# Moving a query projection of a hybrid attention layer from the solve into the attention slots

## The chip, the cores and the metric

The kernel runs on one core of one Trainium2 chip. The metric is device time in microseconds (us) of one execution. The core has a matmul engine (TensorE, in the rows PE, with its weight loads as PEld), VectorE (DVE), ScalarE (ACT) and GpSimd (POOL), and SyncE (SP), whose work here is to issue DMA transfers. Each engine takes its instructions from a queue of its own; semaphores make an instruction wait for one on another engine.

## The reference

The reference runs two layers over 256 latent tokens and 256 context tokens of width 1024. Each layer is half a SwiGLU step, a token mixer, and half a SwiGLU step, each followed by a layer norm. The change touches the mixer of layer 0 alone. That mixer has two groups of heads side by side:

```
h = modulated tokens (512 x 1024)
A (8 heads of 64):  q, k, v = h @ w; rotary on the latent rows of q and k
    latent rows:  softmax over a window of 128 on either side, all context keys, and a sink logit
    context rows: softmax over the context keys and the sink
B (4 heads of 128, forward and backward): q, k, v, z, gates = h @ w
    q, k, v = silu(short_conv(.)) of five taps along the tokens; q and k normalised
    gated delta rule: a state S per head, S <- decay * (S - beta k (k.S)) + beta k v, read out by q
    out = norm(read-out) * silu(z)
x = layernorm(alpha * x + gate * (concat(A, B) @ w_out))
```

All of it is float32 arithmetic.

## The kernel before

**Products.** A float32 matrix is split into a high part (`wh`, `ht_hi`, cast on ACT, or on DVE and POOL) and the remainder (`wl`, `ht_lo`, a subtraction on DVE or POOL). A product is three matmuls: high by high (L391), low by high (L393) and high by low (L394). A projection of 128 columns over 512 tokens is 24 matmuls that fill one PSUM bank.

**Order.** The program is written in Python as a list of operations. A scheduling pass then fixes, before anything runs, the order of the instructions on every engine. So an edit in the source moves instructions on all engines, and within an engine the order stands: what waits holds up all that is behind it. Buffers come from small pools with tags: a projection asks for "a bank with tag pm", gets the oldest, and waits until the last reader of what was in it is done.

**First part of the mixer, `ab_proj`.** PSUM is divided into banks pm (two), x (two), g, q, and r (two). PE computes the k projections of the four B heads (`pproj`, the latent half first, the context half when its transposes are ready), the gate projection (`pg`, 16 rows, in bank g), the four q projections (the first in bank q, the others in pm), and then four z projections. Each k and q projection goes through `ab_conv`: the middle tap on ACT (L901), four taps on DVE (L912), silu on ACT (L916). The bank is free when the last tap is done. The results are transposed on PE (`pkt`, `pqt`), their squares are summed on ACT, and POOL raises the sums to a power (`rk`, `rki`, `rq`, L938). `pgt` is the transpose of the gates. `pG` and `pQ` are the Gram matrices of head 0 (keys by keys, and queries by keys). Between them DVE applies the last layer norm's weight and bias to the rows of the residual (L330, eight operations of 128x1024, tiles r0 and r1), and POOL sends the rows to a store (`xs`), because the space of r0 and r1 is used for the A queries (`qTa`) and keys (`kk`) later.

**Second part, `ab_late`.** The Gram matrices of all heads are weighted and transposed, and go through a store (`scr_out`) into the tile W of DVE, which solves a triangular system in 31 steps of two operations (`ab_solve`, L1177 and L1181, result X). While DVE solves, PE makes the A queries of heads 0 to 3 (`ab_attn_proj(0)`: four steps `pat`, each a product of 128 tokens by 256 columns, a rotary product on DVE and POOL for the latent tokens, a transpose `pqT`), the four v projections (banks g and q in turn) and the A queries of heads 4 to 7 (`ab_attn_proj(1)`). DVE puts the taps of the v convolutions between the solve's steps. Two of the v's have one tap on ACT and POOL (L909, L910). X then goes through a store (`scr_in`) into the tile `xv`.

**Third part.** PSUM is divided anew into banks O (two), sc (two) and dn (four). The A attention runs in 35 pipelined slots (`attn_a`): the query is split on ACT and POOL (`qs`, L1294 and L1295), PE makes scores (`pS`), DVE takes the maximum (L1313), ACT the exponential (L1318), DVE divides (L1322), PE transposes (`pP`, "turn") and multiplies by the values (`pOa`). These slots lie between the steps that turn X into the inverses of the blocks (`delta_inverse`: `pN`, `pZ`, with DVE's transposes `z` of `xv`) and then between the steps of the scan over the tokens (`delta_scan`).

The functions that the change touches:

## Time and profile before

| | us |
|---|---|
| median of three runs | 1801.73 (1801.4 to 1803.04) |
| the profiled execution | 1802.69 |
| its span | 1800.3 |
| PE busy in the span | 1757.1 (98%) |
| DVE busy in the span | 1239.4 (69%) |

Times in the rows count from the start of the span. The span is the part of the execution between the first and the last recorded instruction; 2.4 us lie around it. "PEclk" is the share of PE's full clock that was granted in a stretch: 1.00 is 2.4 GHz, and 0.50 is 1.2 GHz. A number in square brackets behind a row is the time that the engine stood idle before it, and behind the arrow what ended that. A name in the rows is the tile in the program, with the number of the buffer left out.

### The profile page before, as it was taken

The page shows a single profiled execution, that of the slowest core. Times are in us where ns is not written, and L with a number is a line of the kernel's source. Part 1 is how long each engine was busy: PE and PEld are TensorE (multiplying, and loading weights), DVE is VectorE, ACT ScalarE, POOL GpSimd, SP SyncE. Part 2 cuts the span into 40 slices and gives each one's busy share as a digit, 9 for nine tenths or more (in the row PEclk, how much of TensorE's full clock was granted, in tenths as well). Part 3 has the DMA queues.
Part 4 walks back from the last instruction along what each step waited for, and adds up shares of the span by engine and source line. Part 5 has one row for each costly group of instructions (what it writes and reads, how often), then busy time and mean ns, then how long its engine had stood idle before and what let it go on. Part 6 is the DMA issues. An engine that isn't in the chain of part 4 may idle for free. (4 is left out here: it accounts for less than half of the span.)

```text
span 1800.3 us, 24410 instructions
## 1 busy us (share of the span) xinstructions
PE 1757.1 (98%) x9571; PEld 1481.2 (82%) x9571; DVE 1239.4 (69%) x1956; ACT 670.4 (37%) x1176; POOL 180.5 (10%) x296
## 2 busy tenths in 40 slices
PE   6999999999998999999999999999999999999997
PEld 2978878878797988987887888878878889889997
DVE  2784864867778785897674436885756769777556
ACT  2432232224654663342331222522332225655442
POOL 1000000002242310200000002000000023010000
PEclk9999999999999999999999999999999999999999
DMA  9564543623241123375452223662653524146652
GB/s 350 190 211 139 187 164 119 222 60 119 89 125 63 56 77 110 131 244 187 160 169 94 94 96 139 197 223 95 206 192 105 199 81 161 36 162 224 196 177 96
DMA packets 178173, 267.56 MB, mean 149 GB/s; under 512 B 14639, under 2 KB 126683, under 8 KB 177547
## 3 DMA queue, kind: packets, MB, share of 16 engines
q1 hardware_dynamic: 172944, 250.58, 41.9%
q0 software_dynamic: 4624, 14.29, 2.4%
q8 instruction: 75, 1.23, 0.3%
q10 hardware_dynamic: 491, 1.15, 0.2%
q14 instruction: 39, 0.32, 0.1%
HBM read 259.64 MB, written 6.34 MB: 148 GB/s over the span
## 5 line engine op out<-in xcount | busy, mean ns | idle before, releaser
L374 ACT ACTIVATE wh<-wr 128x1024 fp32r<-128x1024 f32 (+1 forms) x311 | 325.4, 1057 | 790.8 <-PE pgu L393 307.0
L376 DVE TENSOR_TENSOR wl<-wr,wh 128x1024 fp32r<-128x1024 f32 (+1 forms) x311 | 375.5, 1219 | 220.8 <-ACT wh L374 217.3
L391 PE MATMUL pgu<-ht_hi,wh 128*128 128x512 f32 (+1 forms) x1472 | 516.1, 353 | 3.5 <-ACT h L266 3.5
L393 PE MATMUL pgu<-ht_lo,wh 128*128 128x512 f32 (+1 forms) x1472 | 518.1, 353 | 0.5 <-POOL ht_lo L269 0.5
L394 PE MATMUL pgu<-ht_hi,wl 128*128 128x512 f32 (+1 forms) x1472 | 517.9, 353 | 0.1
L391 PEld LDWEIGHTS pgu<-ht_hi,wh 128*128 128x128 f32 x1472 | 277.6, 190 | 43.5 <-ACT h L266 3.8
L393 PEld LDWEIGHTS pgu<-ht_lo,wh 128*128 128x128 f32 x1472 | 278.9, 190 | 38.5 <-POOL ht_lo L269 0.9
L394 PEld LDWEIGHTS pgu<-ht_hi,wl 128*128 128x128 f32 x1472 | 278.9, 190 | 37.9 <-DVE wl L376 0.3
L170 DVE SCALAR_TENSOR_TENSOR acc<-wa,cv,acc 128x1024 f32<-128x1024 f32 x224 | 272.8, 1279 | 0.0
L393 PE MATMUL pdn<-wl,hhi 128*128 128x512 f32 (+1 forms) x622 | 240.9, 388 | 0.0
L391 PE MATMUL pdn<-wh,hhi 128*128 128x512 f32 (+1 forms) x622 | 239.9, 390 | 0.0
L394 PE MATMUL pdn<-wh,hlo 128*128 128x512 f32 (+1 forms) x622 | 239.2, 388 | 0.0
L391 PEld LDWEIGHTS pdn<-wh,hhi 128*128 128x128 f32 x622 | 116.6, 188 | 32.4 <-issue 7.5
L394 PEld LDWEIGHTS pdn<-wh,hlo 128*128 128x128 f32 x622 | 116.8, 188 | 23.8
L393 PEld LDWEIGHTS pdn<-wl,hhi 128*128 128x128 f32 x622 | 116.8, 188 | 23.5
L440 DVE TENSOR_TENSOR sg<-sg,pgu 128x512 f32<-128x512 f32 (+1 forms) x86 | 53.6, 623 | 109.0 <-PE pgu L394 105.0
L625 DVE SCALAR_TENSOR_TENSOR tm<-pdn,gate 128x512 f32<-128x512 f32 (+1 forms) x98 | 64.3, 675 | 61.2 <-PE pdn L394 61.1
L439 ACT ACTIVATE sg<-pgu 128x512 f32<-128x512 f32 (+1 forms) x86 | 46.0, 535 | 66.2 <-PE pgu L394 66.2
L198 POOL DMA_DIRECT2D gsc<-rows x12 | 6.2, 524 | 628.0 <-DVE rows L181 628.0
L441 ACT ACTIVATE hhi<-sg 128x512 fp32r<-128x512 f32 (+1 forms) x86 | 49.5, 576 | 35.2 <-DVE sg L440 35.2
L442 DVE TENSOR_TENSOR hlo<-sg,hhi 128x512 fp32r<-128x512 f32 (+1 forms) x86 | 53.6, 624 | 12.2 <-ACT hhi L441 12.2
L394 PE MATMUL pproj<-ht_hi,wl 128*128 128x512 f32 (+1 forms) x160 | 56.1, 355 | 0.0
(383 smaller groups left out, 2203.9 us busy)
## 6 DMA issues: line engine op xcount, KB each, us to landing
wr<-in_ffn_w_gu_dram SPq DMA_DIRECT2D x84, 1024.0 KB
wa<-in_ada_w_dram SPq DMA_DIRECT2D x144, 512.0 KB
wr<-in_ffn_w_down_dram SPq DMA_DIRECT2D x40, 1024.0 KB
wr<-in_ab_w_in_dram SPq DMA_DIRECT2D x11, 1024.0 KB
wr<-in_c_w_in_dram SPq DMA_DIRECT2D x6, 1024.0 KB
gate<-gsc POOLq DMA_DIRECT2D x10, 512.0 KB, 4.9
wr<-in_ffn_w_gu_dram SPq DMA_DIRECT2D x8, 512.0 KB
wr<-in_ffn_w_down_dram SPq DMA_DIRECT2D x8, 512.0 KB
```

Source lines behind the costliest of these rows:

```text
L170: i = nc.vector.scalar_tensor_tensor(out=acc[:, sl], in0=wa[:, sl], scalar=cv, in1=acc[:, sl], op0=ALU.mult, op1=ALU.add)
L198: nc.gpsimd.dma_start(out=self.gsc[m // 3, :, h * 512:(h + 1) * 512], in_=rows[32 * g:32 * g + 2, :])
L374: self.last_high = nc.scalar.activation(out=hv, in_=raw, func=AF.Copy)
L376: self.last_split = (eng or nc.vector).tensor_tensor(out=lv, in0=raw, in1=hv.bitcast(F32), op=ALU.subtract)
L391: self.first_mm = nc.tensor.matmul(out=out, lhsT=lhs[0], rhs=rhs[0], start=start, stop=False)
L393: self.link(nc.tensor.matmul(out=out, lhsT=lhs[0], rhs=rhs[1], start=False, stop=False))
L394: self.last_mm = nc.tensor.matmul(out=out, lhsT=lhs[1], rhs=rhs[0], start=False, stop=stop)
L439: nc.scalar.activation(out=sg, in_=pts[0][:, :NT], func=AF.Silu)
L440: nc.vector.tensor_tensor(out=sg, in0=sg, in1=pts[1][:, :NT], op=ALU.mult)
L441: nc.scalar.activation(out=h_hi[:, c, :], in_=sg, func=AF.Copy)
L442: self.evacuated = nc.vector.tensor_tensor(out=h_lo[:, c, :], in0=sg, in1=h_hi[:, c, :].bitcast(F32), op=ALU.subtract)
L625: i = nc.vector.scalar_tensor_tensor(out=tm, in0=pt[:, cs], scalar=mul, in1=self.gate[:, t // 2, ds], op0=ALU.mult, op1=ALU.mult)
```

## The change

The banks of the four k projections, the places of the eight row operations and of the two transfers to the store, and the last query projection with what hangs on it are moved. No arithmetic is added or taken out. The projection `ab_attn_proj(1)` runs its steps in the order of tokens 2, 3, 0, 1 in banks dn, one behind each of the first four attention slots; its temporaries lie in the tiles of the inverse (`va`, `z`). v3 is written into a part of `qTa`, transposed in a bank dn, and its exponentials' order is set by `last_silu`. The solve's product tile is `sT` instead of one of its own. The attention slots take heads 0 to 3 of two blocks of tokens first, so that the first eight need no query of heads 4 to 7.

```diff
--- before.py
+++ after.py
@@ -913,10 +913,11 @@
                 out=av[:, :, t0:t1], in0=pv[:, :, t0 + o:t1 + o], scalar=w(j), in1=av[:, :, t0:t1],
                 op0=ALU.mult, op1=ALU.add,
             )
-        self.after(nc.scalar.activation(out=dst, in_=a, func=AF.Silu), hold)
-
-    def ab_tok(self, src, name):
-        pt = self.bank("x", name)
+        self.last_silu = nc.scalar.activation(out=dst, in_=a, func=AF.Silu)
+        self.after(self.last_silu, hold)
+
+    def ab_tok(self, src, name, tag="x"):
+        pt = self.bank(tag, name)
         for tb in range(4):
             self.nc.tensor.transpose(
                 out=pt[:, tb * 128:(tb + 1) * 128], in_=src[:, tb * 128:(tb + 1) * 128], identity=self.ident
@@ -993,7 +994,7 @@
         need(3)
         pts = []
         for n in range(4):
-            pts.append(self.bank("r" if n > 1 else "pm", "pproj"))
+            pts.append(self.bank("rrgq"[n], "pproj"))
             self.proj(pts[n], *ws[n], (0, LAT))
         self.start_context()
         for n in range(4):
@@ -1024,9 +1025,10 @@
                 )
             if h == 1:
                 rows()
-            self.next_affine(2, self.convolved)
-            if h % 2:
-                nc.gpsimd.dma_start(out=self.xs[:, h - 1:h + 1], in_=self.rows[h // 2])
+            if h:
+                self.next_affine(2, self.convolved)
+            if h == 2:
+                nc.gpsimd.dma_start(out=self.xs[:, 0:2], in_=self.rows[0])
 
         for h in range(4):
             pt = chunk(9 + h)
@@ -1041,6 +1043,8 @@
                 exps()
             self.ab_gram(h)
             if h == 0:
+                self.next_affine(2, self.weighed)
+                nc.gpsimd.dma_start(out=self.xs[:, 2:4], in_=self.rows[1])
                 self.vt = L.tile([P, 4, 4, P], F32, tag="gate", name="vt", bufs=1)
         self.ab_pow(self.rq, ssq, -0.5)
         V.tensor_scalar(out=self.rq, in0=self.rq, scalar1=float(P) ** -0.5, scalar2=None, op0=ALU.mult)
@@ -1063,8 +1067,8 @@
             for x in range(2):
                 wv.append(self.split_w(raw[:, :, P * x:P * x + P], aw if p else False))
 
-        def v_tok(h):
-            pv = self.ab_tok(vTs[h], "pvt")
+        def v_tok(h, tag="x"):
+            pv = self.ab_tok(vTs[h], "pvt", tag)
             V.tensor_tensor(
                 out=vt[:, :, h, :], in0=pv.rearrange("p (t x) -> p t x", t=4),
                 in1=rki[:, :, h].unsqueeze(2).to_broadcast([P, 4, P]), op=ALU.mult,
@@ -1073,7 +1077,8 @@
         def value(h):
             pt = self.bank("q" if h % 2 else "g", "pproj")
             self.proj(pt, *wv[h], (0, TOK))
-            vTs.append(self.tmp("sq"))
+
+            vTs.append(self.qT[:, 3, :] if h == 3 else self.tmp("sq"))
             self.ab_conv(pt, 8 + h, vTs[h], [self.last_exp], (0,) if h > 1 else ())
             zt = self.tmp("m")
             nc.sync.dma_start(out=zt, in_=self.zscr[h])
@@ -1096,11 +1101,8 @@
                 self.after(self.last_load, [self.W_load])
             value(h)
             self.ab_solve(3)
-        for i, f in enumerate(self.ab_attn_proj(1, weights[1])):
-            f()
-            if i == 0:
-                v_tok(3)
-                self.ab_solve(3)
+        self.ab_solve(3)
+        return weights[1], lambda: v_tok(3, "dn")
 
     def ab_gram(self, h):
 
@@ -1144,7 +1146,7 @@
                     out=self.AT[u][:, tb, :], in0=pG[:, tb * P:(tb + 1) * P], scalar=self.a2[:, tb, u:u + 1],
                     in1=E3[:, tb, :], op0=ALU.mult, op1=ALU.mult,
                 )
-            V.tensor_tensor(out=self.PT[u].rearrange("p t x -> p (t x)"), in0=pQ, in1=E, op=ALU.mult)
+            self.weighed = V.tensor_tensor(out=self.PT[u].rearrange("p t x -> p (t x)"), in0=pQ, in1=E, op=ALU.mult)
             src = self.AT[u]
             if d == 1:
                 sT = self.tmp("sT")
@@ -1173,7 +1175,7 @@
         V, W, X = nc.vector, self.W, self.X
         for j in range(self.solved, min(self.solved + n, 31)):
             m, k = j + 1, 31 - j
-            pv = self.aw.tile([P, 256], F32, tag="prd", name="prd", bufs=1)[:, 0:m * k].rearrange("p (a b) -> p a b", a=m)
+            pv = self.tmp("sT")[:, 0:m * k].rearrange("p (a b) -> p a b", a=m)
             V.tensor_tensor(
                 out=pv, in0=X[:, 0:m, j:j + 1].to_broadcast([P, m, k]),
                 in1=W[:, j:j + 1, j + 1:32].to_broadcast([P, m, k]), op=ALU.mult,
@@ -1197,12 +1199,12 @@
         raw = self.load_w(w[:, :, 256 * p:256 * p + 256])
         return [self.split_w(raw[:, 4 * x:4 * x + 4, :], pool, eng) for x in range(2)]
 
-    def ab_attn_proj(self, p, ws):
+    def ab_attn_proj(self, p, ws, banks=("pm", "x"), tags=("m", "m"), order=range(4)):
 
         nc, io, P = self.nc, self.io, 128
         V = nc.vector
         rope = self.rope
-        tmp = lambda: self.tmp("m")
+        tmp = lambda: self.tmp(tags[0])
 
         def rot(dst, src, tb, n):
 
@@ -1210,7 +1212,7 @@
                 nc.scalar.activation(out=dst, in_=src, func=AF.Copy)
                 return
             co, si = (rope[:, tb, i, :].unsqueeze(1).to_broadcast([P, n, 32]) for i in range(2))
-            t = tmp()
+            t = self.tmp(tags[1])
             t1 = t[:, 0:32 * n].rearrange("p (h x) -> p h x", h=n)
             t2 = t[:, 256:256 + 32 * n].rearrange("p (h x) -> p h x", h=n)
             x1, x2 = src[:, :, 0:32], src[:, :, 32:64]
@@ -1227,7 +1229,7 @@
 
         def step(tb):
             sl = slice(tb * P, (tb + 1) * P)
-            pt = self.bank("pm", "pat")
+            pt = self.bank(banks[0], "pat")
             for k in range(KD):
                 hv, lv = ws[k // 4]
                 self.mm3(
@@ -1239,7 +1241,7 @@
                 rot(q.rearrange("p (h x) -> p h x", h=4), pt[:, 0:256].rearrange("p (h x) -> p h x", h=4), tb, 4)
 
                 def finish(sl=sl, q=q):
-                    pq = self.bank("x", "pqT")
+                    pq = self.bank(banks[1], "pqT")
                     for c in range(2):
                         nc.tensor.transpose(
                             out=pq[:, c * P:(c + 1) * P], in_=q[:, c * P:(c + 1) * P], identity=self.ident
@@ -1269,7 +1271,7 @@
                 done.pop()()
             done.append(finish)
 
-        return [lambda tb=tb: step(tb) for tb in range(4)] + [lambda: done.pop()()]
+        return [lambda tb=tb: step(tb) for tb in order] + [lambda: done.pop()()]
 
     def split_o(self, c, sl, src):
 
@@ -1283,7 +1285,7 @@
 
         nc, P = self.nc, 128
         V = nc.vector
-        items = [(tb, h) for tb in (2, 3, 0, 1) for h in range(8)]
+        items = [(tb, h) for g in ((2, 3), (0, 1)) for h4 in (0, 4) for tb in g for h in range(h4, h4 + 4)]
         state = {}
 
         def query(tb, h):
@@ -1315,7 +1317,8 @@
                 out=st[:, 2:3], in0=st[:, 0:1], scalar=-0.125, in1=self.nsink[:, h:h + 1], op0=ALU.mult, op1=ALU.min
             )
             pe = self.tmp("pexp")[:, 0:nk]
-            nc.scalar.activation(out=pe, in_=s, func=AF.Exp, scale=0.125, bias=st[:, 2:3], accum_out=st[:, 3:4])
+            i = nc.scalar.activation(out=pe, in_=s, func=AF.Exp, scale=0.125, bias=st[:, 2:3], accum_out=st[:, 3:4])
+            self.after(i, [self.last_silu])
             nc.scalar.activation(out=st[:, 4:5], in_=self.sink[:, h:h + 1], func=AF.Exp, bias=st[:, 2:3])
             V.tensor_tensor(out=st[:, 5:6], in0=st[:, 3:4], in1=st[:, 4:5], op=ALU.add)
             V.reciprocal(out=st[:, 6:7], in_=st[:, 5:6])
@@ -1601,12 +1604,19 @@
                     self.ctx_tag, self.lnpool = "x", self.long
                     with self.phase_pool("aw") as self.aw, self.temps(cacc=2, sq=2, sT=1, m=3):
                         self.ab_proj()
-                        self.ab_late(self.aw)
+                        aw, last_values = self.ab_late(self.aw)
                     self.ctx_tag, self.lnpool = "dn", None
-                self.new_ht()
                 st.enter_context(self.psum(O=2, sc=2, dn=4))
                 with self.temps(z=2, va=2, o=3, pexp=3, pT=3):
+
                     att = self.attn_a()
+                    for f in self.ab_attn_proj(1, aw, ("dn", "dn"), ("va", "z"), (2, 3, 0, 1)):
+                        if len(att) > 31:
+                            att.pop(0)()
+                        f()
+                        if last_values:
+                            last_values = last_values()
+                    self.new_ht()
                     inv = self.delta_inverse()
                     for i, f in enumerate(inv):
                         f()
```

On PE, between the k projections' last matmuls and the gate projection. Before (`pproj` first k, then `pg`):

```order
L394 MATMUL pproj<-ht_hi,wl 128x256
L391 MATMUL pproj<-ht_hi,wh 128x256
L393 MATMUL pproj<-ht_lo,wh 128x256
L394 MATMUL pproj<-ht_hi,wl 128x256
L393 MATMUL pg<-ht_lo,wh 16x512
L394 MATMUL pg<-ht_hi,wl 16x512
```

After, on PE at the beginning of the gate projection (the `pproj` rows are the end of q2):

```order
L393 MATMUL pproj<-ht_lo,wh 128x512
L394 MATMUL pproj<-ht_hi,wl 128x512
L922 MATMUL pkt<-ident,skT 128x128 x8
L391 MATMUL pg<-ht_hi,wh 16x512
L393 MATMUL pg<-ht_lo,wh 16x512
L394 MATMUL pg<-ht_hi,wl 16x512
```

The gate projection moved from directly behind the k projections to behind q1, q2 and two key transposes.

On DVE, around the copy of the gates (`gt`) and the taps of q0 and q1 (`cacc`). Before:

```order
L830 COPY gt<-pgt 128x64
L833 TENSOR_TENSOR gy<-gt,hd 128x32
L912 SCALAR_TENSOR_TENSOR cacc<-pproj,cwc,cacc 128x2x254
L834 SCALAR_TENSOR_TENSOR gu<-gy 128x32
L912 SCALAR_TENSOR_TENSOR cacc<-pproj,cwc,cacc 128x2x255
L849 TENSOR_SCALAR gy<-gy 128x32
L376 TENSOR_TENSOR wl<-wr,wh 128x1024
```

After, on DVE at the same copy:

```order
L830 COPY gt<-pgt 128x64
L833 TENSOR_TENSOR gy<-gt,hd 128x32
L1020 TENSOR_TENSOR rk<-rk 128x16
L834 SCALAR_TENSOR_TENSOR gu<-gy 128x32
L838 TENSOR_SCALAR beta<-beta 128x32
L849 TENSOR_SCALAR gy<-gy 128x32
L839 RECIPROCAL beta<-beta 128x32
L1021 TENSOR_TENSOR a_2964<-beta,rk 128x32
L912 SCALAR_TENSOR_TENSOR cacc<-pproj,cwc,cacc 128x2x254 x2
L841 TENSOR_SCALAR gs<-gu 128x32
L912 SCALAR_TENSOR_TENSOR cacc<-pproj,cwc,cacc 128x2x255 x2
```

The square of `rk` moved ahead of the taps of q0 and q1, which now come two and two.

On PE, from the last v projection to the inverse. Before (`pat` and `pqT` are the query projection, `pvt` the transpose of v3):

```order
L394 MATMUL pat<-wh,ht_lo 128x256
L921 MATMUL pvt<-ident,sq 128x128 x4
L1244 MATMUL pqT<-ident,m 128x128 x8
L1511 MATMUL pO_5494<-identR,zeroR 128x512
L1511 MATMUL pO_5537<-identR,zeroR 128x512
L1303 MATMUL pS<-kk,qs 128x256 x6
L1329 MATMUL pP<-ident,pexp 128x128 x2
L1398 MATMUL pN<-z,AT 128x96 x4
```

After, on PE (`pproj` is the end of v3, `pvt` the transpose of v2):

```order
L394 MATMUL pproj<-ht_hi,wl 128x512
L922 MATMUL pvt<-ident,sq 128x128 x4
L1514 MATMUL pO_5603<-identR,zeroR 128x512
L1514 MATMUL pO_5616<-identR,zeroR 128x512
L1305 MATMUL pS<-kk,qs 128x256 x2
L391 MATMUL pat<-wh,ht_hi 128x256
L393 MATMUL pat<-wl,ht_hi 128x256
```

The four steps of the projection moved from between the v projections to behind the scores of the first slot; the other three steps follow one slot each.

## Rows read from the trace of the kernel before

**Rows 1.** The page, busy time of each engine.
```profile
PE 1757.1 (98%) x9571; PEld 1481.2 (82%) x9571; DVE 1239.4 (69%) x1956; ACT 670.4 (37%) x1176; POOL 180.5 (10%) x296
```

**Rows 2.** Busy time by stretch: us, PE, PEld, DVE, ACT, POOL, clock, DMA.
```profile
464.00:467.00 3.00, 0.00 (x0) 0.00 (x0) 3.00 (x5) 2.97 (x5) 0.94 (x1) 0.84 0.01 3
467.00:473.00 6.00, 5.90 (x20) 5.15 (x21) 5.74 (x10) 2.51 (x11) 6.00 (x2) 0.51 0.58 175
```

**Rows 3.** Busy time by stretch, later in the mixer.
```profile
500.00:510.00 10.00, 10.00 (x70) 8.94 (x69) 8.21 (x20) 6.87 (x20) 3.92 (x9) 1.00 0.51 147
...
520.00:530.00 10.00, 10.00 (x87) 9.92 (x86) 8.57 (x22) 7.94 (x25) 3.18 (x9) 1.00 0.10 16
...
570.00:580.00 10.00, 7.09 (x44) 5.55 (x44) 7.17 (x25) 4.59 (x14) 4.28 (x8) 0.93 0.13 52
580.00:590.00 10.00, 6.81 (x34) 6.29 (x34) 5.36 (x18) 4.73 (x14) 7.28 (x17) 0.56 0.20 34
```

**Rows 4.** PE's waits, 560 to 600 us: total, times, longest.
```profile
PE pP L1329 <- DVE pexp L1322: 3.3, 1, 3.3
PE pat L391 <- DVE m L1223: 1.5, 1, 1.5
PE pS L1303 <- POOL qs L1295: 1.2, 1, 1.2
PE pqT L1244 <- ACT qTa L1247: 0.8, 2, 0.6
PE pN L1398 <- DVE z L1390: 0.3, 1, 0.3
```

**Rows 5.** PE in order of time, 440 to 468 us: start, duration.
```profile
440.40 0.39 PE L393 MATMUL pg<-ht_lo,wh 128*16 128x512 f32 x1
...
445.03 0.40 PE L393 MATMUL pproj<-ht_lo,wh 128*128 128x512 f32 x1
...
462.90 1.05 PE L1117 MATMUL pG<-skT 128*128 128x128 f32 x8
467.10 1.12 PE L921 MATMUL pqt<-ident,sqT 128*128 128x128 f32 x4 [3.15 <-ACT sqT L916]
```

**Rows 6.** ACT in order of time, around k0's silu.
```profile
446.89 1.28 ACT L916 ACT_TABLE_LOAD   x1 [5.06 <-issue]
448.19 0.63 ACT L916 ACTIVATE skT<-cacc 128x512 f32<-128x512 f32 x1
```

**Rows 7.** DVE in order of time, a weight difference and eight taps.
```profile
438.81 1.23 DVE L376 TENSOR_TENSOR wl<-wr,wh 128x1024 fp32r<-128x1024 f32 x1 [3.97 <-ACT wh L374]
...
449.58 5.59 DVE L912 SCALAR_TENSOR_TENSOR cacc<-pproj,cwc,cacc 128x508 f32<-128x508 f32 x8 [1.31 <-ACT cacc L901]
```

**Rows 8.** POOL in order of time, the three powers.
```profile
466.06 5.06 POOL L938 TENSOR_TENSOR rk<-ssk,mhalf 128x16 f32<-128x16 f32 x1 [30.56 <-DVE ssk L1008]
471.09 2.90 POOL L938 TENSOR_TENSOR rki<-ssk,phalf 128x16 f32<-128x16 f32 x1
...
489.35 2.92 POOL L938 TENSOR_TENSOR rq<-ssq,mhalf 128x16 f32<-128x16 f32 x1 [3.96 <-DVE ssq L1040]
```

**Rows 9.** DVE in order of time: v0's last tap, v2's, X's last step, z.
```profile
548.46 0.74 DVE L912 SCALAR_TENSOR_TENSOR cacc<-pproj,cwc,cacc 128x508 f32<-128x508 f32 x1
...
562.54 0.73 DVE L912 SCALAR_TENSOR_TENSOR cacc<-pproj,cwc,cacc 128x508 f32<-128x508 f32 x1
...
576.50 0.21 DVE L1181 TENSOR_TENSOR X<-X,prd 128x31 f32<-128x31 f32 x1
...
583.11 0.71 DVE L1390 STREAM_TRANSPOSE z<-xv 128x512 f32<-128x512 f32 x1
```

**Rows 10.** PE: start of v2, one `pat` step's stretch, first scores behind the inverse's start.
```profile
550.73 0.40 PE L391 MATMUL pproj<-ht_hi,wh 128*128 128x512 f32 x1
...
570.37:573.32 2.95, 2.95 (x24) 1.00 0.00 0
...
588.96 0.49 PE L1303 MATMUL pS<-kk,qs 128*128 128x256 f32 x2
```

## The prediction, made before the changed kernel ran

> **What bounds the kernel now.** I read the page's engine table first: the matmul engine (PE) is busy 98% of a span of 1800.3 us [rows 1]. A change can therefore only win in the few stretches in which PE idles or runs at the lower clock, and it loses wherever it opens a new one. Next I read the busy time by stretch around the mixer of layer 0. Two holes show. At 464 to 467 us PE does nothing for 3 us, and from 467 to 473 us it is busy, but the granted clock is 0.51, which is the 1.2 GHz level [rows 2]. At 570 to 590 us PE is busy 7.09 and then 6.81 us in ten, and the clock falls to 0.56 [rows 3]. The list of PE's waits says what ends the second hole: 3.3 us for the softmax of the first slots, 1.5 us for a rotary product, 1.2 us for the query split on POOL, 0.8 and 0.3 us for small things, 7.1 us in all [rows 4]. With the clock (0.07 of 7.09 and 0.44 of 6.81, so 3.5 us) the hole costs 10.6 us, and that is the most that filler could win there. The first hole costs 3.15 us of waiting [rows 5] and half of the six slow microseconds, 2.9 us.
>
> **The change, first place: the key projections' banks.** The four k projections now take the two r banks, g and q; so q1 and q2 (banks pm) follow directly, and the gate projection (bank g) must wait for k2's convolution, q0 (bank q) for k3's. The work is the same, so I follow when PE arrives at the same point.
>
> Before, the k projections end at 440.40, twenty 512-column matmuls then take 4.63 us (0.23 each), and pG ends at 463.95; PE waits till 467.10 for q0's silu [rows 5]. At 467.10 all of gates, q0, q1, q2, four key transposes and pG is done.
>
> After, eight matmuls of pg and q0 no longer stand among the k projections. At 0.23 they are 1.8 us; they filled places where the transposed context comes piecemeal, so I count 1.3. The k's end at 439.1; q1 and q2 take 48 times 0.23, two key transposes 0.4 each (half of pG's eight): 451.0. Now pg needs k2's convolution. ACT has one weight cast more in front of the silu table load, and that cast waits for q1's last high-part product (444.4). So cast 1.0, table load 1.28, silu 0.63, then k2's first tap about 0.6 [rows 6]: DVE may start on k2 at 448.2. In DVE's order k2's last tap is the seventh entry: six taps at 0.69 (5.59 over eight) and one weight difference of 1.13 [rows 7], so 453.5. PE idles 2.5 us.
>
> Then pg 5.6, two transposes 0.8, q0 5.6, pgt 0.4 and pG 0.9 bring PE to 466.8. Its next item is q3, in q1's bank. q1 was done at 444.7, but its convolution now stands on DVE behind the copy of pgt (465.1) and behind rk*rk, which waits for POOL's power; both convolutions' eight taps come interleaved after that. q0's first tap can start at about 466.2; eight taps and three small gate operations take 6.1 us: 472.3. PE idles 5.5 us, then runs slow as it does now after 3.15 us of idling.
>
> So PE is at the same point, with the same slow restart behind it, at 472.3 instead of 467.10: **+5.2 us**. Behind it PE has no idle to give it back: the stretches at 500 and 520 us show 10.00 of 10 [rows 3]. Bounds: if the clock does not fall, 2.9 less (+2.3). If the first new idle also costs six slow microseconds, 2.9 more (+8.1).
>
> The power decides a part of this. The three powers on POOL took 5.06, 2.90 and 2.92 us [rows 8]. The first ran beside busy DVE, but so did the second; the third ran in a lull. I take 2.9 for the changed kernel (the nearest row is the third, since DVE then waits), which hides the power; with 5.06 the chain ends at 473.4, that is +6.3.
> The Trainium skill (GPSIMD Engine Reference, "Specifications") says that POOL shares its memory interface with VectorE and is held up by VectorE instructions with two inputs in that memory. By that rule the power takes 2.9 here and the term is +5.2; by "the first one is long" it is +6.3. The trace does not bear the rule out, for the 2.90 us one had such instructions beside it too.
>
> **Second place: the affine rows.** The eight row operations stay eight. Two now stand on DVE around gram 0's transpose, and the copy of r1 to its store leaves only then, on POOL's queue; the keys in r1's space wait for it, but the scores want them some 60 us later. DVE is busy 8.21 and 8.57 of 10 there [rows 3]. Each costs about what the weight difference costs that has its shape, 1.2 [rows 7], so there is room for both and I cost them at 0. If they delay every gram to the last one, the solve starts 2.4 us late.
>
> **Third place: the last query projection.** Before, its four steps fill PE between the v projections; a step of 24 matmuls takes 2.95 us, 11.8 in all [rows 10]. After, PE's order is v0, v1, v2, v3 in a row, then pvt, the pO clears, slot 0's scores, and only then the first projection step. Now each v must wait for its bank. In before's times: v2 starts at 550.73 behind a projection [rows 10]; now it starts when v0's last tap is done, 549.1 [rows 9], and PE idles 1.6 from 547.6. v2 and v3 with a transpose each end at 561.2. v2's last tap ended at 563.2 before [rows 9]; with v2 1.5 earlier I take 562.2, silu 0.63 [rows 6], and PE idles 1.7. After pvt and pO, at 563.8, slot 0's scores need its query, cast on ACT behind v3's silu, behind v3's last tap. On DVE that comes after five solve operations (2.1), one vt (0.6), three taps (2.1) and two more solve operations (0.7): 567.7. Silu, cast and POOL's difference make it 569.0, so PE idles 5.2. In all 8.5 us against 7.1: **+1.4**. From 569 PE has some 15 us of work in a row (four steps, pvt, four scores, two turns, three transposes) before the inverse.
>
> The solve itself ends earlier: before, X's last step is done at 576.7 and z follows at 583.11 [rows 9], 6.4 later. Without eight rotary operations (1.6) and without v3's vt (0.6 and its wait) X ends at about 574, so z could be ready at 580.5. But PE arrives there only at 569 + 15 + 2.9 (slow restart) = 587. The wait for z is gone and PE's own queue is late instead. The clock loses 2.9 instead of 3.5: **-0.6**. At the point that before reaches at 588.96 [rows 10], scores, turns and one product of later slots have been done that before did afterwards, at 0.15 to 0.5 us each: **-1.2**. Together -0.4. Bounds: -3.3 if the clock does not fall, +2.5 if the new small waits in that row of work (transposes for rotary products, turns for exponentials) cost what such waits cost now, 1.1 us, and the scan later lacks the slots that were taken out (1.4 us).
>
> **Sum.** 5.2 + 0 - 0.4 = +4.8. The profiled execution took 1802.69 us, so 1807.5 there; it lies 0.96 over the median of 1801.73, so I predict a median of **1806.5**.
>
> **Rivals.**
> *The second wait of the first place does not arise.* q1 is ready 20 us before its convolution is wanted. If its taps are done by 466.8, PE goes from pG into q3 without a stop: -0.3 there, and no slow restart, -2.9. With the third place at -0.4 to -3.3 that is -3.6 to -6.5, some 1796.5. For it: by the working above DVE has little to do between k3's last tap (about 455) and pgt (465). Against it: DVE takes its instructions in order, and the taps stand behind rk*rk. It decides at the end of q1's last tap, 466.8.
> *The waits come, but the clock stays up.* First place +2.3, third -0.4: 1803.6, no difference that counts. For it: waits of 1.5 and 1.2 us in the second hole left the clock at 0.93 on average over 570:580 [rows 3, 4]. Against it: 3.15 us were enough at 464 [rows 2, 5], and mine are 5.
> *Both idles are followed by slow stretches and the grams are late too.* +8.1, +2.4, and +1: 1813.
> *The projection fills the hole as it is meant to.* It would be worth up to 10.6 us. It needs the steps to run while DVE solves; they stand behind slot 0's scores, which wait for v3's silu, so only the end of the solve is covered. I count it in the first rival.
>
> **Chances.** Forecast 0.38, the two idles with slow stretches and late grams 0.10, clock stays up 0.29, first rival 0.23. A measurement of this kernel tells 0.2% (3.6 us) from no change. So faster 0.23, no change 0.29, slower 0.48. The range, with a tenth left out at either end, reaches from the first rival to short of the worst case: 1796 to 1812; the forecast's own range is 1805.4 to 1810.
>
> **What would show it.** The gate projection starting 2 to 3 us after q2's end with a release by a tap on DVE; q3 starting at about 472 with the same releaser, and a clock near half behind it; the matmul that stood at 467.10 about 5 us later. Then PE idle for 5 us before slot 0's scores, released by POOL, and no wait for z. It is wrong if q3 follows pG at once, if PE has no idle between the v projections and slot 0, or if the inverse starts earlier, counted from v1's end, than now.

## The result, and the profile after

The changed kernel takes 1814.16 us (median of 4 executions, 1812.95 to 1817.79), the kernel before on the same chip 1801.57 (4 executions). The ratio is 1.0068 with an interval of 1.0055 to 1.0080: about 12 us slower. The prediction was 1806.5, with a range from 1796 to 1812. The sign and the place of most waits were right, the size was too small by more than half.

TensorE (PE) is as busy as before, and the work is the same, so the 12.1 us between the two spans (1812.4 and 1800.3) must be idle time and lower clock. The page's row for the engines [rows 1] is now:

```profile
PE 1755.3 (97%) x9571; PEld 1479.9 (82%) x9571; DVE 1243.1 (69%) x1956; ACT 670.0 (37%) x1176; POOL 177.7 (10%) x296
```

For the places I use the busy time by stretch (length, PE's busy time, granted clock, DMA). First in four long stretches of the profile after:

```profile
430.00:535.00 105.00, 96.49 (x567) 0.97 0.30 95
535.00:620.00 85.00, 72.92 (x493) 0.92 0.26 82
620.00:735.00 115.00, 114.69 (x848) 1.00 0.23 74
735.00:790.00 55.00, 52.30 (x330) 0.97 0.48 160
```

The length of a stretch less PE's busy time is idle time. The busy time multiplied by one less the granted clock is what the lower clock costs. Both are summed over short stretches of 2.5 us, because a long stretch mixes the two levels of the clock. The two kernels then compare so (us of idle + us lost to the clock, from one execution of each):

| stretch | before | after | more |
|---|---|---|---|
| 430-535, first hole | 3.2 + 2.8 | 8.5 + 1.7 | +4.2 |
| 535-620, second hole | 7.3 + 3.3 | 12.1 + 4.5 | +6.0 |
| 620-735, scan | 0.9 + 0.0 | 0.3 + 0.0 | -0.6 |
| 735-790, next half-step | 0.3 + 0.0 | 2.7 + 1.5 | +3.9 |
| behind that | 4.6 + 1.7 | 4.8 + 0.0 | -1.5 |

The sum is +12.0. The table leaves out what lies ahead of 430 us, where the changed kernel has 1.6 us more, most of it idle in the first 40 us, which the change does not touch. So the account is good to about 2 us. The short stretches, as in [rows 2, 3], show where:

```profile
450.00:460.00 10.00, 7.27 (x39) 1.00 0.34 107
460.00:470.00 10.00, 7.38 (x40) 0.98 0.00 0
470.00:480.00 10.00, 6.86 (x27) 0.68 0.00 1
550.00:560.00 10.00, 6.96 (x23) 0.75 0.23 79
560.00:570.00 10.00, 10.00 (x45) 0.91 0.16 53
570.00:580.00 10.00, 2.57 (x13) 0.77 0.07 26
580.00:590.00 10.00, 9.77 (x73) 0.89 0.23 69
747.00:757.00 10.00, 7.56 (x50) 0.83 0.68 224
```

550 to 560 us was full before and is now a third idle at a clock of 0.75. The same stretch of the kernel before:

```profile
550.00:560.00 10.00, 10.00 (x58) 1.00 0.08 29
```

PE's waits in the changed kernel, 424 to 800 us (total, times, longest), beside [rows 4]:

```profile
PE pproj L391 <- DVE cacc L912: 8.8, 2, 5.8
PE pS L1305 <- POOL qs L1297: 5.5, 1, 5.5
PE pg L391 <- DVE cacc L912: 2.7, 1, 2.7
PE pgu L391 <- DVE tm L625: 2.4, 1, 2.4
PE pvt L922 <- ACT sq L916: 1.9, 1, 1.9
PE pN L1401 <- DVE z L1393: 1.4, 1, 1.4
```

The same waits with their times, from PE's timeline (start, duration, in brackets the idle before and its releaser), beside [rows 5, 10]:

```profile
453.83 0.40 PE L391 MATMUL pg<-ht_hi,wh 128*16 128x512 f32 x1 [2.73 <-DVE cacc L912]
...
473.14 0.77 PE L391 MATMUL pproj<-ht_hi,wh 128*128 128x512 f32 x1 [5.76 <-DVE cacc L912]
...
498.37 0.72 PE L1126 MATMUL pr<-gr,sel 64*128 64x512 f32 x2
...
555.69 0.76 PE L391 MATMUL pproj<-ht_hi,wh 128*128 128x512 f32 x1 [3.04 <-DVE cacc L912]
...
572.67 0.66 PE L922 MATMUL pvt<-ident,sq 128*128 128x128 f32 x4 [1.93 <-ACT sq L916]
...
579.29 0.80 PE L1305 MATMUL pS<-kk,qs 128*128 128x256 f32 x2 [5.50 <-POOL qs L1297]
...
597.06 1.13 PE L1401 MATMUL pN<-z,AT 128*128 128x96 f32 x8 [1.38 <-DVE z L1393]
...
749.63 0.55 PE L391 MATMUL pgu<-ht_hi,wh 128*128 128x256 f32 x1 [2.44 <-DVE tm L625]
```

In order: the gate projection, q3, the first gram's row matmul, v2, v2's transpose, slot 0's scores, the inverse, the gate-up projection of the next half-step. VectorE (DVE) at the solve's start and at three of these places, beside [rows 7, 9]:

```profile
540.87 0.19 DVE L1179 TENSOR_TENSOR sT<-X,W 128x31 f32<-128x31 f32 x1 [1.98 <-issue]
...
553.67 1.22 DVE L376 TENSOR_TENSOR wl<-wr,wh 128x1024 fp32r<-128x1024 f32 x1
554.80 0.74 DVE L912 SCALAR_TENSOR_TENSOR cacc<-pproj,cwc,cacc 128x508 f32<-128x508 f32 x1
...
564.06 0.69 DVE L1072 TENSOR_TENSOR vt<-pvt,rki 128x512 f32<-128x512 f32 x1 [3.35 <-PE pvt L922]
564.67 0.41 DVE L1179 TENSOR_TENSOR sT<-X,W 128x256 f32<-128x256 f32 x1
...
583.48 0.22 DVE L1183 TENSOR_TENSOR X<-X,sT 128x31 f32<-128x31 f32 x1
...
596.11 0.28 DVE L1225 TENSOR_TENSOR z<-pat,ropea 128x128 f32<-128x128 f32 x1
596.30 1.53 DVE L1393 STREAM_TRANSPOSE z<-xv 128x512 f32<-128x512 f32 x2
```

In the kernel before, the first gram's row matmul and the solve's first step stood here:

```profile
493.46 0.72 PE L1124 MATMUL pr<-gr,sel 64*128 64x512 f32 x2
```

```profile
535.31 0.19 DVE L1177 TENSOR_TENSOR prd<-X,W 128x31 f32<-128x31 f32 x1 [1.80 <-DMA W<-scr_out]
```

And two of the three powers on POOL [rows 8], of which the first took 5.06 us before:

```profile
462.77 2.92 POOL L939 TENSOR_TENSOR rk<-ssk,mhalf 128x16 f32<-128x16 f32 x1 [27.87 <-DVE ssk L1009]
465.65 2.90 POOL L939 TENSOR_TENSOR rki<-ssk,phalf 128x16 f32<-128x16 f32 x1
```

One chain in the middle is worth following. v0's last tap now stands behind a weight difference (553.67), so v2 waits 3.04 us for its bank and runs at the lower level of the clock (0.50 from 555 to 560 us). The transpose of v0 is queued behind v2 and comes at 563.4. VectorE stands still 3.35 us for it, and the next step of the solve (564.67) stands behind the waiting instruction although it needs nothing from it. X's last step starts at 583.48, 7.0 later than before [rows 9]. The solve's first step comes 5.6 later (535.31 before, 540.87 now), and from there the solve takes 1.4 longer.

### The profile page after: what moved, and what is told of

Its sections match the earlier page's. It is cut to its first block, busy times and chain, and to the rows that moved or that the text cites. A ratio compares the mean times of both kernels' runs of the same rounds, so it can differ in the third digit from the quotient of the medians.

```text
span 1812.4 us, 24412 instructions
## 1 busy us (share of the span) xinstructions
PE 1755.3 (97%) x9571; PEld 1479.9 (82%) x9571; DVE 1243.1 (69%) x1956; ACT 670.0 (37%) x1176; POOL 177.7 (10%) x296
## 5 line engine op out<-in xcount | busy, mean ns | idle before, releaser
L391 PE MATMUL pproj<-ht_hi,wh 128*128 128x512 f32 (+1 forms) x160 | 56.8, 367 | 9.0 <-DVE cacc L912 8.8
```

The costliest lines, as they stand in the source:

```text
L391: self.first_mm = nc.tensor.matmul(out=out, lhsT=lhs[0], rhs=rhs[0], start=start, stop=False)
```

## The experiments

The theory after the comparison: the loss is three separate waits, the first hole, v2's bank, and the bank at the next half-step. The rivals: one late arrival makes the others late, or the solve on VectorE decides whatever PE does. All ratios are to executions of the kernel before on the same chip; the difference in us is that ratio less one, times its median. The difference between two kernels that were each set against the kernel before carries both intervals, some 3 us either way where each ratio has 0.0012. What is said of single stretches comes from one execution of each kernel.

**One part done or undone.**

```
before_new_banks      before, and  bank("r" if n > 1 else "pm") -> bank("rrgq"[n])
after_old_k_banks     after, and   bank("rrgq"[n]) -> bank("r" if n > 1 else "pm")
after_old_affine      after, and   if h: next_affine / if h == 2: dma   -> next_affine / if h % 2: dma
                                   - next_affine(2, self.weighed), its dma   (rows as before)
```

> The kernel before with one edit: the four k projections take the banks r, r, g, q. Theory (three separate waits add up, and this is the first): +4.9 us, as measured between the traces at the first gram; the gate projection starts about 453.8 after an idle of about 2.7, q3 about 473.1 after an idle of about 5.8, and the rest is pushed by the same 5 us: 1806.5. Rival (one cause: this wait makes all that comes after late): the whole of the loss, about +12.6: 1814. Rival (the later holes absorb it): within 2 us of the kernel before.

Measured: 1.0061 (1.0049 to 1.0074), +11 us. That is far more than the first place's 5, but it is not the price of the first place alone, as the order of instructions shows below.

> The changed kernel with the k projections back in pm, pm, r, r. Theory (the waits add up): -4.9 us, so 1809.3, with v2's wait near 3 us, slot 0's near 5.5 us and the wait at the start of the next half-step near 2.4 us all still there. Rival (one cause): back to about 1802, and those later waits shrink.

Measured: 1.0035 (1.0023 to 1.0047), +6.3, so -6.0 against the changed kernel, which is near the theory's -4.9. But the later waits changed: v2 waited 1.2, and a projection step waited behind a softmax:

```profile
581.01 0.58 PE L391 MATMUL pat<-wh,ht_hi 128*128 128x256 f32 x1 [5.60 <-ACT pexp L1320]
```

> The changed kernel with the row operations back at two per convolved key head and their stores with them. Theory (the second part costs nothing): within 1 us of the changed kernel, 1814. Rival (two of the eight ops on VectorE between the grams delay the solve's start): the solve starts 0.6 to 2.4 us earlier and as much is won, 1812 to 1813.5.

Measured: 1.0126 (1.0112 to 1.0140), +22.7: 10 us slower than the changed kernel. Neither theory had this. The order of the instructions on PE gives most of the reason. With both parts old or both new, 89 or 86 matmuls of the first attention projection stand ahead of the last gram on PE; with new rows and old banks (after_old_k_banks) 135, with new banks and old rows (after_old_affine and before_new_banks) 162. At 0.123 us each (2.95 for 24, [rows 10]) that puts 5.7 and 9.3 us more work ahead of the last gram, and the solve starts behind it: at 540.96 with old banks, though the first hole is back at 3.9 us of idle, and at 554.96 with old rows, against 540.87 in the changed kernel. Of these last 14.1 us, 9.3 are the order and 3.6 a deeper first hole (9.8 + 4.0). The two parts are a pair; an experiment that takes one of them measures another order.

**The pair, and the move, each alone.**

```
before_first_two_parts   before, with the new k banks and the new rows
after_third_part_alone   after, with the old k banks and the old rows
```

> The kernel before with the new k banks and the new places of the row operations, and the last query projection where it was. In the built order the grams then stand where they stand in both shown kernels (86 of the attention projection's matmuls ahead of the last one; 135 or 162 when only one of the two parts is made). Theory (the first two parts belong together and cost what the first place shows, 5.3 us more idle and 1.1 less at the lower clock): about +4.2 us on the kernel before, 1806.5 to 1807.5, with the second hole as before (7.3 us idle, 3.3 lost to the clock). Rival (the late arrival makes the second hole deeper): +8 to +12.

> The changed kernel with the old k banks and the old places of the row operations: the last query projection's move alone. Theory (the move itself deepens the second hole from 10.6 to about 16.6 us of TensorE time and brings the wait at the next half-step, 2.4 idle and 1.5 at the lower clock): about +8 to +10 us on the kernel before, 1811 to 1813, with the first hole as before. Rival (the second hole was deep only since the first place came late): +3 to +5.

Measured: the pair 1.0056 (1.0044 to 1.0068), +10.1; the move alone 1.0012 (1.0003 to 1.0020), +2.2. Neither theory's figure came: the pair costs more than was expected of it and the move less. Together they make 12.3, which is the changed kernel's difference. The pair's account: first hole 8.8 + 3.9, second 7.8 + 3.9, scan 0.9 + 3.4, next half-step 0.3 + 0.0, later 4.6 + 0.0. So the second hole is only 1.1 deeper. The first hole costs +6.7 instead of the +4.2 in the changed kernel, for the most part because the gate projection's wait is followed here by a clock of 0.66 (455 to 460 us), where the changed kernel has 1.00. And a slow stretch opens in the scan, where PE pauses 0.4 us in all, as it does before at a full clock. The pair was profiled in a second execution:

> A second profiled execution of the kernel before with the first two parts of the change. The first one lost 3.4 us to the lower clock in the scan (640 to 650 us at 0.66), behind pauses of 0.4 us in all that the kernel before has too. If the stretch belongs to the kernel, it shows again at the same place; if the lower clock there comes and goes between executions of one program, this one is without it, and its span is about 3 us nearer to 1808.

The slow stretch came again at the same place, on another chip, so it belongs to the kernel (1814.44 us in this execution). The first hole came to 9.1 + 5.2 this time, 1.6 more than in the first execution: so much can differ between two executions of one program. The row of the first profile, then that of the second:

```profile
640.00:650.00 10.00, 10.00 (x60) 0.66 0.18 69
```

```profile
640.00:650.00 10.00, 9.84 (x53) 0.66 0.32 107
```

What lowers the clock there is not shown. before_new_banks has the same loss of 3.4 in the scan; the changed kernel has none.

The move alone: first hole 3.3 + 1.6, second 9.7 + 2.7 (before 7.3 + 3.3), next half-step 2.7 + 1.6, later 4.6 + 0.0 (before 4.6 + 1.7). PE and VectorE at the start of the chain:

```profile
548.96 0.47 PE L391 MATMUL pproj<-ht_hi,wh 128*128 128x512 f32 x1 [1.56 <-ACT cacc L901]
```

```profile
554.57 0.69 DVE L1069 TENSOR_TENSOR vt<-pvt,rki 128x512 f32<-128x512 f32 x1 [0.35 <-PE pvt L922]
```

v2 waits 1.56, the 1.6 of the prediction, and VectorE's stall is 0.35. (The row names a tap on ACT as the releaser; it ends at 548.83, v0's last tap on DVE at 548.81.) The weight difference stands behind v0's last tap here, and the solve runs from 534.90 to 574.40. So the chain of 3.04, lower clock and 3.35 needs both parts. Of the +6.0 in the changed kernel's second hole the move alone brings 1.8 and the pair alone 1.1, which leaves some 3 us that exist only with both. The +2.2 of the move is a small sum of larger terms: +4.0 at the next half-step and +1.8 in the second hole, against 1.1 less in the first hole, 0.6 less in the scan, and a slow stretch of 1.7 further on that the kernel before has and this one does not.

**Single waits of the changed kernel.**

```
after_sc_first        + self.bank("sc"), self.bank("sc")        ahead of  att = self.attn_a()
after_v_in_r_banks    bank("q" if h % 2 else "g") -> bank("gqrr"[h])              in value(h)
after_step_first      the loop over the steps:  f(); last_values;  then  att.pop(0)()
```

> The changed kernel with the two sc banks of the attention stage claimed before its first slot, so that they lie where they lay before and the next half-step's first gate-up bank was not last held by a block of the output projection. Nothing else is moved. Theory (a bank is what is waited for): the wait of 2.44 us on the multiply of the output projection's block goes, the slow stretch behind it too, so -3.9 us: 1810.3. Rival (the start of the half-step waits because VectorE itself is late there): the wait stays under another name, 1814.

Measured: 1.0048 (1.0035 to 1.0060), 3.6 us less than the changed kernel, and the next half-step's hole fell from 2.7 + 1.5 to 1.1 + 0.0:

```profile
747.43 0.38 PE L391 MATMUL pgu<-ht_hi,wh 128*128 128x256 f32 x1 [0.87 <-ACT h L266]
```

The wait on the output projection's block is gone; what is left is another operand. The theory holds for the wait; the 3.6 us in the time stand against an uncertainty of about 3. The banks' numbers are read from the built program, no trace shows them: the attention stage's banks are given out at first use. Before, its two sc banks were banks 0 and 1, and the next half-step's gate-up tiles take 0, 2 and 1. In the changed kernel slot 0 and the steps ask first, dn gets 0 to 3, and bank 0 last holds a block of the output projection.

> The changed kernel with v2 and v3 in the two r banks, so that they need not wait for the convolutions of v0 and v1. Theory (v2's bank wait starts a cascade: 3.04 us idle, half clock, a late transpose, and 3.35 us in which VectorE stands still in the middle of the solve): v2 follows v1 at once, VectorE's stall shrinks from 3.35 to about 0.7 as in the kernel before, slot 0 starts 3 us earlier, X ends 3 us earlier: -3 to -6 us, 1808 to 1811. Rival (slot 0's wait for v3's convolution takes up whatever is won): X ends when it did, 1814.

Measured: 1.0049 (1.0037 to 1.0061), 3.4 less. VectorE's stall is gone and X ends 39.1 us behind the solve's first step instead of 42.6; but slot 0 still waits, and a softmax is waited for instead:

```profile
PE pS L1305 <- POOL qs L1297: 5.2, 1, 5.2
PE pat L391 <- ACT pexp L1320: 2.1, 1, 2.1
```

The second hole is 10.1 + 4.6 instead of 12.1 + 4.5: the theory's cascade is there, and the rival takes back about a third of the 3.04. The rest of the 3.4 us is not placed by the stretches: the next half-step has 1.5 less at the lower clock in this execution, and the first hole 1.3 more.

> The changed kernel with only the order in the loop turned: the projection's step ahead of the slot. Theory (slot 0's scores at the head of the queue keep ready work waiting): the idle ahead of slot 0's scores falls from 5.5 to about 2.5 us or less, -2 to -3 us: 1811 to 1812. Rival (the solve's end decides): the inverse's first matmul moves by less than 1.4 us and its wait for z grows to 3 or 4 us: about 1813.

Measured: 1.0071 (1.0058 to 1.0083), no gain. The second hole fell to 9.3 + 3.0, 4.3 us less, as the theory has it; the first hole lost 1.4 more in that execution and the next half-step's wait grew to 3.0. What is won ahead of slot 0 was not seen in the time.

**Mending together.**

```
after_three_undone              old k banks, "gqrr" for v, sc banks claimed first (new rows kept)
after_three_undone_step_first   the same, and the step ahead of the slot
third_part_sc_first_step_first  the move alone, sc banks claimed first, the step ahead of the slot
third_part_all_mended           the same, and "gqrr" for v
```

> The changed kernel with three of its placements undone together: k projections back in pm, pm, r, r; v2 and v3 in the r banks; the two sc banks claimed first. One at a time these measured -6.0, -3.4 and -3.6 us against the changed kernel (by the ratios to the kernel before of the same runs). Theory (three separate waits): they add up to -13, so this kernel lies within 2 us of the kernel before, with the last query projection still behind slot 0. Rival (the waits stand one behind the other, and VectorE's solve decides the middle): the two first overlap, -8 at most, so about 4 us slower than the kernel before.

> As the run with three placements undone, and in the loop over the last query projection each step is recorded ahead of the slot instead of behind it, so that TensorE's queue holds 24 ready matmuls in front of slot 0's scores. Theory (slot 0's scores at the head of the queue keep ready work waiting): the first step, 2.95 us, moves into the idle of 5 us, so 2 to 3 us less than the run without it: about 1 to 3 us faster than the kernel before. Rival (the end of the solve decides when the inverse starts, z was already waited for 1.4 us): at most 1.4 us less, and the wait for z grows by the rest.

> The last query projection's move alone, with the two sc banks claimed first and each projection step recorded ahead of the slot. Theory: the hole at the next half-step goes (-3.6), and the turned order wins 2 to 4 us of the idle ahead of slot 0: about +2 us on the kernel before, 1803 to 1806. Rival (what is won comes back as a wait for a softmax or for z): as the move alone less 3.6, +5.

> The same with v2 and v3 in the two r banks. Theory (v2's wait of 3 us was idle that counts): 2 to 3 us less than the run without it, equal to the kernel before or 1 us faster: 1801 to 1803. Rival (TensorE only comes earlier to VectorE's chain, as it did where three placements were undone): no less than the run without it.

Measured: 1.0033 (1.0022 to 1.0045), 1.0019 (1.0010 to 1.0029), 0.9996 (0.9987 to 1.0004) and 0.9992 (0.9983 to 1.0001). The single gains did not add up in the first (+5.9, its second hole is 14.9 + 4.3, for the mixed order starts the solve late); the second, with the loop turned, measured 2.5 less, but the two intervals overlap. With old rows and banks the mended move is level with the kernel before, not measurably faster.

**Other banks for the steps.**

```
after_steps_in_sc_banks      after, and  ab_attn_proj(1, aw, ("dn", "dn"), ..) -> ("sc", "dn")
mended_steps_in_sc_banks     third_part_all_mended with ("sc", "dn"), without the claiming line
mended_sc_banks_turn_in_va   third_part_all_mended with ("sc", "dn") and tags ("va", "va")
```

> The changed kernel with one edit: the four steps of the last query projection take the attention stage's two sc banks instead of its dn banks. In the built order 66 of their matmuls (8.1 us at 0.123 each) then stand ahead of slot 0's scores instead of none; the first of them waits for a convolution. Theory (what stands ahead of slot 0 in TensorE's queue decides whether the 5.5 us are filled): that idle falls by 4 us or more and its slow stretch with it: -4 to -6 us, 1808 to 1810. Rival (the end of the solve decides when the inverse starts): the idle comes back ahead of the inverse or of a softmax: within 2 us of 1814.

> The move alone, with v2 and v3 in the r banks, each step ahead of the slot, and the steps in the sc banks (which claims these banks first by itself, so the line that did so is gone). 82 of the steps' matmuls stand ahead of slot 0's scores. Theory: of the 8.0 us idle and 2.2 lost to the clock that the kernel with all mended still shows there, the 4.1 us in front of the first step go and the slow stretch behind them: -4 to -6 us, so 1795 to 1797, faster than the kernel before by more than 0.2%. Rival (the end of the solve decides): 1799 to 1801.

> The same with the rotary products of the steps in the va buffers alone, so that no z buffer is held by a step when the inverse wants its transposed blocks, and the sc banks claimed by the line as before. Theory (z stands behind the last step's rotary products in VectorE's order; that was the wait of 1.4 us that the prediction did not have): the inverse's first matmul no longer waits for z behind a step: 1 us less than with the z buffers. Rival (the va buffers are wanted by the inverse as well, and the wait only changes its name): the same or slower.

Measured: 1.0087 (1.0070 to 1.0104), 0.9996 (0.9987 to 1.0005), 0.9995 (0.9986 to 1.0004). The first is slower although the wait at slot 0 is gone: the next half-step now waits 6.02 us (6.3 + 2.5 in that stretch), and the second hole is 9.0 + 7.2.

```profile
754.26 0.55 PE L391 MATMUL pgu<-ht_hi,wh 128*128 128x256 f32 x1 [6.02 <-DVE tm L625]
```

In the second, 82 ready matmuls stand ahead of slot 0, and its hole is 7.4 + 4.7 against 8.0 + 2.2. The waits, 545 to 605 us:

```profile
PE pP L1329 <- DVE pexp L1322: 2.2, 1, 2.2
PE pvt L922 <- ACT qTa L916: 2.0, 1, 2.0
PE pvt L922 <- ACT sq L916: 1.5, 1, 1.5
PE pqT L1243 <- POOL va L1223: 1.4, 1, 1.4
```

PE comes earlier and waits for the softmax, for silus and for rotary products: the rival's side. Moving the rotary products out of the z buffers changed nothing that can be measured. The wait for z that it was to take away was 0.3 us in mended_steps_in_sc_banks already, and with the change an inverse's matmul (`pN`) waited 2.1 us for VectorE's reduction of a slot's scores (L1313).

## Why the prediction was too small

**First place: right in place, near in size in the changed kernel, in part by luck.** 2.5 and 5.5 us of idle were predicted, 2.73 and 5.76 came, with the releasers named; q3 started at 473.14 (predicted 472.3), the first gram's row matmul moved by 4.9. Both powers took 2.9, as I took them. Inside the changed kernel the stretch costs +4.2 (predicted +5.2), since the slow part behind it is shorter, 1.7 for 2.8. That depends on the clock behind the gate projection's wait, which stayed at 1.00 in this execution. In the pair it fell, and the same place cost +6.7 and +8.3 in two executions; the prediction has this case as its upper bound, +8.1, and did not take it. Nor did it have the 3.4 us that the pair alone loses in the scan some 170 us later.

**Second place: the time of the operations is nil, their effect is not.** I costed them by their durations and their room on VectorE. Put back, they cost 10 us, for the order of PE's instructions hangs on them. With the new banks the new rows stand well, so as a term of the changed kernel the 0 did no harm that can be seen. But the first two places were priced as two separate terms, and the runs show that they are one.

**Third place: this is the step that failed, "Together -0.4".** Its stretch and what follows came to 6.0 - 0.6 + 3.9 = +9.3 (behind that, 1.5 less than before). The step was worked out "In before's times", as if the first two places only shift what comes behind them. The move alone shows what that was worth: without the first two places v2 waits 1.56 (predicted 1.6) and X is done at 574.6 (predicted about 574). With them the order on VectorE is another, and the waits grow. Term by term:
- The waits were predicted as 1.6, 1.7, 5.2 and none for z (8.5); they were 3.04, 1.93, 5.50 and 1.38 (11.9). For v2 I took the time of the last tap from the profile before, shifted, without the weight difference that now stands ahead of it: 1.4 more.
- "The wait for z is gone": z's transpose stands behind the rotary products of the last step in VectorE's order (596.11, 596.30), so it could not be ready ahead of PE: 1.4. The move alone has this wait too.
- "The clock loses 2.9 instead of 3.5": it loses 4.5 (the kernel before 3.3 by the sum over short stretches), for v2's wait has a slow stretch of its own.
- X was to end "at about 574", shifted by the first hole 579; its last step started at 583.48. PE's delay came back to VectorE as the 3.35 us in front of vt. I had followed PE waiting for VectorE and not VectorE waiting for PE. The Trainium skill (PSUM — Partial Sum Buffer, "Engine vs sequencer instructions") says that VectorE's queue is strictly first in, first out; the trace agrees, the solve's step at 564.67 stood behind vt.
- The next half-step's first bank, 2.44 us of idle and 1.5 at the lower clock, was not in the sum at all. The renumbering of banks is a part of the change that I followed to the end of the stage and not into the next one. after_sc_first puts its price at 3.6, give or take 3.

The upper bound of this place has a slip: -0.4 with 1.1 and 1.4 added is +2.1, not +2.5. It does not touch the sum.

**By parts the miss divides otherwise.** The first two places made alone cost +10.1 where 5.2 + 0 was predicted, the move alone +2.2 where -0.4 was. By that count 4.9 of the miss goes with the first two places and 2.6 with the move; by stretches of the changed kernel nearly all of it lies behind the first hole. Both are measured. They differ because the pair alone loses 2.5 more in the first hole and 3.4 in the scan, to the clock in the main, and the changed kernel loses some 3 in the second hole that neither part has alone. A sum of separate terms could not give this.

**The rivals.** The one with both idles slow, 1813, came nearest in time, but in the profiled execution for a reason that it did not name: the slow stretches came behind v2 and at the next half-step, not behind the gate projection. That one came in the pair and in other kernels with the same first place.

**Open:** the lower clock in the scan of the pair, and why the same wait, of 2.75 us ahead of the gate projection or of 2.43 us ahead of the gate-up projection, is followed by the lower clock in one kernel and not in another (below).

## What to carry to other kernels

Where a change renames buffers or banks, list for every instruction behind it what last held its bank, up to the next stage's first tiles; the dearest wait that was missed lay 170 us behind the edit. Where a change has several parts, do not add prices that were each worked out in the old kernel's times: here a wait of 1.6 us became 3.04 because another part had turned the order on VectorE. When an engine is delayed, follow the delay back to whoever queues behind its result, in their order, before the sum is made. Where the order of instructions is built and not written, undoing a part gives another order: look at the order before reading its time.

## What the runs showed of the hardware

The gate projection waited 2.75 us in after_sc_first and in after_v_in_r_banks, with the same instructions on PE in the same order from 436 us up to q3's wait. Behind it the clock stayed at 1.00 in the first and fell in the second:

```profile
454.35 0.40 PE L391 MATMUL pg<-ht_hi,wh 128*16 128x512 f32 x1 [2.75 <-DVE cacc L912]
```

```profile
455.00:460.00 5.00, 5.00 (x25) 1.00 0.61 204
```

```profile
455.19 0.58 PE L391 MATMUL pg<-ht_hi,wh 128*16 128x512 f32 x1 [2.75 <-DVE cacc L912]
```

```profile
455.00:460.00 5.00, 4.81 (x15) 0.66 0.66 213
```

A wait of 2.43 us in front of the same matmuls of the gate-up projection was followed by the lower clock in after_old_k_banks and not in after_v_in_r_banks. It ended at 747.25 in the first and at 750.30 in the second. The stretch behind it, in the first and in the second:

```profile
750.00:755.00 5.00, 5.00 (x37) 0.82 0.38 104
```

```profile
750.00:755.00 5.00, 4.70 (x39) 1.00 0.65 224
```

And in the scan of the pair the clock fell to 0.66 behind pauses of 0.4 us in all, at the same place in two executions, where the kernel before, with the same pauses, has 1.00. The length of the pause alone does not tell whether the clock falls.

The power of 128x16 elements on POOL took 2.92 us in the changed kernel where it had taken 5.06 before. In the 18 profiled executions 44 of the 54 powers took 2.90 to 2.93 us, and ten took 3.22 to 5.06. Each of these ten ran beside two of the row operations on VectorE (L330), none of the other 44 beside more than one. That the row operations hold the power up is not shown by this, for a longer power also meets more of them.
